# A hybrid decoder layer on one core: other SBUF addresses for the activation tiles of its second part

## The chip, the core and the metric

The kernel runs on one core of a Trainium2 chip. A core has five engines with instruction queues of their own: TensorE (PE in the profile; PEld is its loading of weights), VectorE (DVE), ScalarE (ACT), GpSimd (POOL) and SyncE (SP), which here issues all DMAs. The metric is the device time of one execution in microseconds. Three runs of the kernel before took 3090.01, 3095.93 and 3096.91 us, a median of 3095.93 us.

## What is computed

One layer of a decoder with two groups of heads side by side, on 2048 tokens of width 1024, in float32:

```
u = rmsnorm(h, attn_norm_g);  z = u @ w_in             # 2048x1024 @ 1024x3592
y = concat(mlstm_mixer(z parts), diff_attn_mixer(z parts))
h = h + y @ w_out                                      # 1024x1024
u2 = rmsnorm(h, mlp_norm_g)
h = h + square(relu(u2 @ w_up)) @ w_down               # 1024x4096, 4096x1024
gate = sigmoid(rmsnorm(h, ple_norm_g) @ w_ple_gate)    # 1024x1024
h = h + gate * (p @ w_ple_proj)                        # 256x1024
```

## The kernel before

The program has two parts. `phase1` computes z, the two mixers and, at its end, the product with w_out for the first 512 tokens. `phase2` does the rest in two halves (`hf`) of 1024 tokens, each as two column blocks (`j`) of 512 tokens: the product with w_out, the up and down products of the MLP, the gate.

**Matmuls.** Each float32 operand is split into a rounded part "hi" and a rest "lo" (`split`, L70 to L72: ScalarE writes hi, VectorE or POOL writes lo). `mm3` (L130 to L135) multiplies a pair with three matmuls: L133 hi by hi, L134 weight hi by activation lo, L135 weight lo by activation hi. Every matmul loads 128x128 weights anew and streams its moving operand, in `phase2` 512 columns of an activation tile. One output block takes 24 such matmuls (8 pairs), in the down product 12.

**Tiles.** `cut(buf, base, ...)` takes a piece of a large buffer from element `base` on, 4 bytes each. In `phase2` the weights are pieces of `wbuf` whose blocks of 128 columns lie 512 B apart (L848, L849, L867 to L872). An activation tile is 2 x 512 elements, hi then lo, 4096 B. There are 16 for U (`U_r`) and 16 for act: two in `wbuf` behind the weights, six in `act_r`, eight in `ubuf`. A `Ring` hands them out in turn. U tiles are taken for m, j in that order, so an even number holds column block j = 0 and an odd one j = 1. The `gap` of 96 elements (L851) puts `act_r` and `U_r` at the same address modulo 512 B as `wbuf`; `ubuf` and `wbuf` itself stand so already. By the addresses of the built program, the difference (address of the moving operand less address of the weights that are loaded meanwhile, modulo 512 B) is 0 for every matmul of 512 unbroken columns.

In `phase1` it varies. Its weights are in `wbuf` too, in tiles of 528 elements (2112 B) with two blocks of 264 elements (1056 B) in each. Its `trn` uses them as weights against 4 blocks of 128 columns of U in `ubuf` (768 matmuls, L133 to L135, `bank<-ubuf,wbuf`, until about 1205 us); its `nat` uses U as weights and streams 256 columns of them (`bank<-wbuf,ubuf`).

**Order.** The order of instructions on each engine is set by a scheduler at build time, which works by a timeline of its own; each engine then runs its own list in order. `act_r`, `U_r` and the h tiles lie where `phase1` had its working tiles, so they can be written when those are done; the first write to `act_r` follows the last store of y at 1309 us. The first half's y tiles (L916 to L920, for j = 1 alone, eight of them) are loaded through three temporary buffers (`tmp`) that `fin` (L883) uses too.

Of the kernel before, what the change touches and what calls it, by code (L numbers as in the profile page):

```python
# [8 lines left out]
F32R = mybir.dt.float32r  # L9
# [7 lines left out]
P = 128  # L17
# [6 lines left out]
T1 = 512  # L24
# [16 lines left out]
def hybrid_block(ctx: ExitStack, tc: tile.TileContext, a: dict, out: bass.AP):  # L41
# [48 lines left out]

    phase1(tc, a, wbuf, ubuf, rbuf, banks, yT, hd, qkdr, vdr, ident, identr, identb, masks, ones, negh, split, rstd_col, spread)
    phase2(tc, a, wbuf, ubuf, rbuf, banks, yT, hd, out, split, rstd_col, spread)


def cut(buf, base, *dims, cast=None):
    n = 1
    for d in dims:
        n *= d
    t = buf[:, base:base + n]
    if cast:  # L100
        t = t.bitcast(cast)
    if len(dims) == 2:
        t = t.rearrange("p (a b) -> p a b", a=dims[0])
    elif len(dims) == 3:
        t = t.rearrange("p (a b c) -> p a b c", a=dims[0], b=dims[1])
    return t
# [732 lines left out]
def phase2(tc, a, wbuf, ubuf, rbuf, banks, yT, hd, out, split, rstd_col, spread):  # L839
    nc = tc.nc  # L840
    NJ = T2 // T1
    with ExitStack() as ctx:
        pool = lambda name, bufs=1, **k: ctx.enter_context(tc.tile_pool(name=name, bufs=bufs, **k))
        pc = pool("p2")
# [4 lines left out]
        pw.put("lo", [cut(wbuf, i * 2048 + 1024, KT, P) for i in range(3)])  # L849
        pt.put("tmp", [rbuf[:, 2048 + i * T1:2048 + (i + 1) * T1] for i in range(3)])  # L850
        pc.tile([P, 96], F32, name="gap")  # L851
        more = pc.tile([P, 6, 2 * T1], F32R, name="act_r")
        us = pc.tile([P, 16, 2 * T1], F32R, name="U_r")
        pact.put("U", [cut(us[:, i], 0, 2, T1) for i in range(16)])
        pact.put("act", [cut(wbuf, 6144 + i * 1024, 2, T1) for i in range(2)] + [cut(more[:, i], 0, 2, T1) for i in range(6)] +
                 [cut(ubuf, i * 1024, 2, T1) for i in range(8)])
        acc2 = pc.tile([P, T1], F32, name="acc2")
        pacc.put("acc2", [acc2, rbuf[:, 3584:4096]])
# [48 lines left out]
        for hf in range(NT2):  # L907
# [14 lines left out]
            H, U = [], []  # L922
# [162 lines left out]
```

## Time and profile before

| | us |
|---|---|
| median of three runs | 3095.93 |
| the profiled execution | 3100.62 |
| its span, first to last instruction | 3098.8 |
| TensorE busy | 2979.3 |
| VectorE, ScalarE, POOL busy | 1732.1, 1251.6, 1121.5 |
| mean granted TensorE clock | 0.989 of 2.4 GHz |

The span is divided by the stage tables below in us from its start: `phase2` begins at about 1306 us, its first half ends at about 2063 us and the second half's product with w_out at about 2186 us. The time from one matmul's start to the next one's is shorter than a matmul's printed duration, since matmuls overlap; it is read from the starts of many.

### The profile page before, as it was taken

The page shows a single profiled execution, that of the slowest core. Times are in us where ns is not written, and L with a number is a line of the kernel's source. Part 1 is how long each engine was busy: PE and PEld are TensorE (multiplying, and loading weights), DVE is VectorE, ACT ScalarE, POOL GpSimd, SP SyncE. Part 2 cuts the span into 40 slices and gives each one's busy share as a digit, 9 for nine tenths or more (in the row PEclk, how much of TensorE's full clock was granted, in tenths as well). Part 3 has the DMA queues.
Part 4 walks back from the last instruction along what each step waited for, and adds up shares of the span by engine and source line. Part 5 has one row for each costly group of instructions (what it writes and reads, how often), then busy time and mean ns, then how long its engine had stood idle before and what let it go on. Part 6 is the DMA issues. An engine that isn't in the chain of part 4 may idle for free.

```text
span 3098.8 us, 42670 instructions
## 1 busy us (share of the span) xinstructions
PE 2979.3 (96%) x16136; PEld 2537.9 (82%) x16136; DVE 1732.1 (56%) x3426; ACT 1251.6 (40%) x2836; POOL 1121.5 (36%) x802
## 2 busy tenths in 40 slices
PE   7898999999899999999999999999999999999999
PEld 7788888888888888778888888878788888888877
DVE  7888767667767657375433334463454444333462
ACT  4477666667566666342221211231432222211231
POOL 6667535235533322362222222252632222222341
PEclk9899999999999999999999999999999999999999
DMA  5655534334533332431111111214311111111111
GB/s 162 186 171 158 170 113 123 107 99 125 156 101 104 98 103 75 144 130 49 48 48 48 48 48 48 62 39 137 123 48 48 49 53 49 48 48 48 62 48 68
DMA packets 197806, 278.34 MB, mean 90 GB/s; under 512 B 15584, under 2 KB 145120, under 8 KB 197600
## 3 DMA queue, kind: packets, MB, share of 16 engines
q1 hardware_dynamic: 197600, 275.61, 29.3%
q8 instruction: 127, 2.08, 0.3%
q14 instruction: 79, 0.65, 0.1%
HBM read 235.71 MB, written 39.85 MB: 89 GB/s over the span
## 4 chain that ended last, share of the span: by engine, by line
PE 73%; DVE 13%; ACT 4%; DMA 4%; issue 3%; POOL 3%; SPq 0%; POOLq 0%; ACTq 0%; DVEq 0%
PE bank L133 21%; PE bank L134 21%; PE bank L135 21%; PE bank L824 2%; DMA rbuf<-in_w_in_dram 2%; DVE PP_r L800 2%; PE bank L776 1%; PE bank L779 1%; DVE mxp_r L780 1%; DVE U_r L72 1%; PE bank L812 1%; ACT PP_r L788 1%; POOL wbuf L72 1%; DMA rbuf<-in_x_in_dram 1%; DVE qn_r L727 1%
## 5 line engine op out<-in xcount | busy, mean ns | idle before, releaser
L72 POOL TENSOR_TENSOR wbuf<-rbuf,wbuf 128x512 fp32r<-128x512 f32 (+3 forms) x408 | 733.0, 1802 | 1557.8 <-ACT wbuf L71 1522.5
L71 ACT ACTIVATE wbuf<-rbuf 128x512 fp32r<-128x512 f32 (+3 forms) x410 | 325.9, 799 | 794.5 <-PE bank L134 664.9
L133 PE MATMUL bank<-U_r,wbuf 128*128 128x512 f32 x1280 | 500.0, 391 | 11.9 <-ACT U_r L71 5.8
L134 PE MATMUL bank<-U_r,wbuf 128*128 128x512 f32 x1280 | 499.7, 390 | 1.0 <-DVE U_r L72 1.0
L135 PE MATMUL bank<-U_r,wbuf 128*128 128x512 f32 x1280 | 500.1, 391 | 0.0
L133 PE MATMUL bank<-wbuf,ubuf 128*128 128x256 f32 (+1 forms) x1280 | 382.2, 299 | 18.0 <-DVE wbuf L246 5.6
L973 DVE TENSOR_TENSOR h_r<-bank,h_r 128x512 f32<-128x512 f32 x256 | 176.6, 690 | 394.7 <-PE bank L135 394.7
L133 PE MATMUL bank<-ubuf,wbuf 128*128 128x512 f32 x960 | 380.5, 397 | 5.1 <-ACT ubuf L71 2.7
L135 PE MATMUL bank<-ubuf,wbuf 128*128 128x512 f32 x960 | 377.8, 394 | 0.0
L134 PE MATMUL bank<-ubuf,wbuf 128*128 128x512 f32 x960 | 377.7, 393 | 0.0
L134 PE MATMUL bank<-wbuf,ubuf 128*128 128x256 f32 (+1 forms) x1280 | 375.5, 294 | 1.4 <-DVE wbuf L247 0.9
L135 PE MATMUL bank<-wbuf,ubuf 128*128 128x256 f32 (+1 forms) x1280 | 374.7, 293 | 0.5 <-DVE ubuf L72 0.5
L133 PEld LDWEIGHTS bank<-U_r,wbuf 128*128 128x128 f32 x1280 | 240.7, 188 | 65.4 <-ACT U_r L71 7.0
L134 PEld LDWEIGHTS bank<-U_r,wbuf 128*128 128x128 f32 x1280 | 240.5, 188 | 52.0 <-DVE U_r L72 1.3
L135 PEld LDWEIGHTS bank<-U_r,wbuf 128*128 128x128 f32 x1280 | 240.4, 188 | 50.6 <-issue 1.2
L133 PEld LDWEIGHTS bank<-wbuf,ubuf 128*128 128x128 f32 x1280 | 251.6, 197 | 24.9 <-ACT qn_r L717 5.6
L952 DVE TENSOR_TENSOR rbuf<-rbuf 128x512 f32<-128x512 f32 x64 | 156.5, 2445 | 206.6 <-ACT rbuf L951 206.5
L134 PEld LDWEIGHTS bank<-wbuf,ubuf 128*128 128x128 f32 x1280 | 251.4, 196 | 4.7 <-DVE wbuf L247 1.5
L135 PEld LDWEIGHTS bank<-wbuf,ubuf 128*128 128x128 f32 x1280 | 251.1, 196 | 2.8 <-DVE ubuf L72 0.5
L780 DVE TENSOR_REDUCE mxp_r<-bank 128x1 f32<-128x512 f32 (+3 forms) x320 | 187.0, 602 | 66.7 <-PE bank L779 65.6
L133 PEld LDWEIGHTS bank<-ubuf,wbuf 128*128 128x128 f32 x960 | 181.1, 189 | 45.4 <-ACT ubuf L71 3.9
L788 ACT ACTIVATE PP_r<-bank,mx_r 128x512 f32<-128x512 f32 (+3 forms) x320 | 196.4, 624 | 47.1 <-DVE mx_r L785 42.5
(243 smaller groups left out, 5401.4 us busy)
## 6 DMA issues: line engine op xcount, KB each, us to landing
rbuf<-in_w_in_dram SPq DMA_DIRECT2D x208, 256.0 KB, 2.8
rbuf<-in_w_up_dram SPq DMA_DIRECT2D x64, 512.0 KB, 3.6
rbuf<-in_w_down_dram SPq DMA_DIRECT2D x64, 512.0 KB, 3.5
KT_r<-qk_d SPq DMA_DIRECT2D x40, 512.0 KB, 5.4
qk_d<-kst_r SPq DMA_DIRECT2D x64, 256.0 KB, 3.0
QT_r<-qk_d SPq DMA_DIRECT2D x128, 128.0 KB, 3.8
rbuf<-in_x_in_dram SPq DMA_DIRECT2D x31, 512.0 KB, 4.0
rbuf<-in_w_out_dram SPq DMA_DIRECT2D x24, 512.0 KB, 4.1
```

The costliest lines, as they stand in the source:

```text
L71: nc.scalar.activation(hi, raw, AF.Copy)
L72: eng.tensor_tensor(out=lo, in0=raw, in1=hi.bitcast(F32), op=ALU.subtract)
L133: nc.tensor.matmul(ps, lhsT=lh, rhs=rh, start=(start and i == 0), stop=False)
L134: nc.tensor.matmul(ps, lhsT=lh, rhs=rl, start=False, stop=False)
L135: nc.tensor.matmul(ps, lhsT=ll, rhs=rh, start=False, stop=(stop and i == n - 1))
L727: nc.vector.tensor_tensor(out=qn, in0=qg, in1=rn.unsqueeze(2).broadcast_to([P, 4, 64]), op=ALU.mult)
L780: nc.vector.tensor_reduce(out=mxp[:, m, ci:ci + 1], in_=Sp[:, 0:n], op=ALU.max, axis=AX.X)
L788: nc.scalar.activation(pp[:, 0:n], sps[ci][:, 0:n], AF.Exp, bias=mx[:, m:m + 1], scale=0.125, accum_out=lp[:, m, ci:ci + 1])
L800: nc.vector.scalar_tensor_tensor(out=A[:, 0:n], in0=PP[1][ci][:, 0:n], scalar=sc[:, 0:1], in1=A[:, 0:n], op0=ALU.mult, op1=ALU.add)
L824: nc.tensor.matmul(po, lhsT=ats[kb // 4][:, (kb % 4) * P:(kb % 4 + 1) * P], rhs=VV[kb // 4][:, kb % 4], start=(kb == 0), stop=(kb == i))
L952: nc.vector.tensor_tensor(out=t, in0=t, in1=R[j], op=ALU.mult)
L973: nc.vector.tensor_tensor(out=H[m][j], in0=p, in1=H[m][j], op=ALU.add)
```

## The change

The act tiles in `wbuf` go; `act_r` takes eight instead of six, and `ubuf` keeps its eight. The tiles in `act_r` and `U_r` get offsets in elements: U 16 for even tiles and 64 for odd ones, act 80 for even and 104 for odd ones, which is 64, 256, 320 and 416 B. In the built program the differences of the 7680 matmuls of `phase2` proper are 64 B (1920, U of j = 0), 256 B (1920, U of j = 1), 320 and 416 B (960 each) and 0 (1920, act tiles in `ubuf`). To make room, the scratch for DMA descriptors at the bottom of SBUF shrinks from 16384 to 1024 B, and all tiles move down by 15360 B.

```
-        more = pc.tile([P, 6, 2 * T1], F32R, name="act_r")
-        us = pc.tile([P, 16, 2 * T1], F32R, name="U_r")
-        pact.put("U", [cut(us[:, i], 0, 2, T1) for i in range(16)])
-        pact.put("act", [cut(wbuf, 6144 + i * 1024, 2, T1) for i in range(2)] + [cut(more[:, i], 0, 2, T1) for i in range(6)] +
+        more = pc.tile([P, 8 * 1024 + 128], F32R, name="act_r")
+        us = pc.tile([P, 16 * 1024 + 128], F32R, name="U_r")
+        pact.put("U", [cut(us, (i % 2) * 8192 + (i // 2) * 1024 + (16, 64)[i % 2], 2, T1) for i in range(16)])
+        pact.put("act", [cut(more, (i % 2) * 4096 + (i // 2) * 1024 + (80, 104)[i % 2], 2, T1) for i in range(8)] +
                  [cut(ubuf, i * 1024, 2, T1) for i in range(8)])
...
-    nc = bacc.Bacc("TRN2", target_bir_lowering=False, num_devices=1)
+    nc = bacc.Bacc("TRN2", target_bir_lowering=False, num_devices=1, dynamic_dma_scratch_size=1024)
```

Since the first two act tiles no longer lie in `wbuf`, the scheduler orders the border between the two parts anew. SyncE's list there, as a difference of the changed kernel from the one before (L917 loads a y tile, L529 and L932 x, L870 and L512 weights, L930 h):

```order
@@ -406,7 +406,5 @@
 L710 DMA yT_d_75<-yo_r 128x512
 L536 DMA h_d<-rbuf 128x512
-L917 DMA rbuf<-yT_d_74 128x512
 L529 DMA rbuf<-in_xT_dram 128x512
-L917 DMA rbuf<-yT_d_74 128x512
 L512 DMA rbuf<-in_w_out_dram 128x1024
 L536 DMA h_d<-rbuf 128x512
```

Two loads of y leave the end of `phase1`.

Further on in SyncE's list:

```order
@@ -442,4 +440,5 @@
 L930 DMA h_r<-h_d 128x512
 L932 DMA h_r<-in_xT_dram 128x512
+L917 DMA rbuf<-yT_d_74 128x512 x2
 L870 DMA rbuf<-in_w_out_dram 128x1024
 L930 DMA h_r<-h_d 128x512
```

They come back behind loads of h and ahead of the next weights.

PE at the border, in the kernel before, where the first three output blocks (banks 66, 67 and 68) begin:

```order
6682 L133 MATMUL bank_67<-act_r,wbuf 128x512
6683 L135 MATMUL bank_68<-wbuf 128x512
6684 L133 MATMUL bank_68<-wbuf 128x512
6685 L134 MATMUL bank_68<-wbuf 128x512
6686 L135 MATMUL bank_68<-wbuf 128x512
6687 L133 MATMUL bank_68<-act_r,wbuf 128x512
```

and in the changed one:

```order
6658 L135 MATMUL bank_68<-ubuf,wbuf 128x512
6659 L495 MATMUL bank_67<-ident,ya_r 128x128
6660 L133 MATMUL bank_66<-act_r,wbuf 128x512
6661 L133 MATMUL bank_67<-act_r,wbuf 128x512
6662 L133 MATMUL bank_68<-act_r,wbuf 128x512
6663 L134 MATMUL bank_66<-act_r,wbuf 128x512
```

Before, 18 matmuls of these blocks read y tiles in `wbuf`; now all 72 read `act_r`.

## Rows read from the trace of the kernel before

**Rows 1.** The page: its head, PE's busy time, the chain by engine
```profile
span 3098.8 us, 42670 instructions
...
PE 2979.3 (96%) x16136; PEld 2537.9 (82%) x16136; DVE 1732.1 (56%) x3426; ACT 1251.6 (40%) x2836; POOL 1121.5 (36%) x802
...
PE 73%; DVE 13%; ACT 4%; DMA 4%; issue 3%; POOL 3%; SPq 0%; POOLq 0%; ACTq 0%; DVEq 0%
```

**Rows 2.** Busy time by stage: stretch, length, each engine's busy time, clock, DMA
```profile
1400.00:2062.00 662.00, 662.00 (x2922) 548.15 (x2921) 283.07 (x324) 148.89 (x207) 162.48 (x75) 1.00 0.16 49
...
2300.00:2974.00 674.00, 674.00 (x2975) 558.12 (x2974) 289.22 (x330) 153.03 (x212) 164.99 (x76) 1.00 0.16 49
```

**Rows 3.** Timeline of PE, second part: start us, duration us, engine, line, operation
```profile
1999.79 0.39 PE L133 MATMUL bank<-ubuf,wbuf 128*128 128x512 f32 x1
...
2009.99 0.39 PE L133 MATMUL bank<-ubuf,wbuf 128*128 128x512 f32 x1
```

**Rows 4.** PE's lines from 1999 to 2060 us: busy us, mean ns, idle us before
```profile
L133 PE MATMUL bank<-act_r,wbuf 128*128 128x512 f32 x45 | 17.5, 389 | 0.0
```

**Rows 5.** Timeline of PE, first part: a stretch of wide matmuls, first and last
```profile
495.42 0.40 PE L134 MATMUL bank<-ubuf,wbuf 128*128 128x512 f32 x1
...
500.07 0.40 PE L133 MATMUL bank<-ubuf,wbuf 128*128 128x512 f32 x1
```

**Rows 6.** Timeline of PE after a stall in the second part
```profile
2087.96 0.39 PE L133 MATMUL bank<-U_r,wbuf 128*128 128x512 f32 x1
...
2090.04 0.39 PE L133 MATMUL bank<-U_r,wbuf 128*128 128x512 f32 x1
```

**Rows 7.** PE's lines at 487.20 us, difference 0: mean ns
```profile
L134 PE MATMUL bank<-ubuf,wbuf 128*128 128x512 f32 x1 | 0.4, 389 | 0.0
```

**Rows 8.** PE's lines at 881.12 and 881.50 us, difference 64 B
```profile
L135 PE MATMUL bank<-ubuf,wbuf 128*128 128x512 f32 x1 | 0.4, 394 | 0.0
L133 PE MATMUL bank<-ubuf,wbuf 128*128 128x512 f32 x1 | 0.4, 388 | 0.0
...
L134 PE MATMUL bank<-ubuf,wbuf 128*128 128x512 f32 x1 | 0.4, 392 | 0.0
```

**Rows 9.** PE's lines at 879.30 us, difference 160 B; L134 and L135 read as in rows 8
```profile
L133 PE MATMUL bank<-ubuf,wbuf 128*128 128x512 f32 x1 | 0.4, 391 | 0.0
```

**Rows 10.** Timeline of PE: first and last wide matmul at 64 (modulo 256), at 160
```profile
396.40 0.40 PE L135 MATMUL bank<-ubuf,wbuf 128*128 128x512 f32 x1
...
1201.21 0.39 PE L135 MATMUL bank<-ubuf,wbuf 128*128 128x512 f32 x1
...
394.32 0.39 PE L135 MATMUL bank<-ubuf,wbuf 128*128 128x512 f32 x1
...
1199.59 0.39 PE L134 MATMUL bank<-ubuf,wbuf 128*128 128x512 f32 x1
```

**Rows 11.** Timeline of VectorE at the border: splits of the first half's y tiles
```profile
1248.58 0.68 DVE L72 TENSOR_TENSOR wbuf<-rbuf,wbuf 128x512 fp32r<-128x512 f32 x1
...
1312.30 1.90 DVE L72 TENSOR_TENSOR act_r<-rbuf,act_r 128x512 fp32r<-128x512 f32 x3 [4.98 <-ACT act_r L71]
...
1319.31 1.43 DVE L72 TENSOR_TENSOR act_r<-rbuf,act_r 128x512 fp32r<-128x512 f32 x2 [5.12 <-ACT act_r L71]
```

**Rows 12.** Timeline of PE at the border, in brackets what it waited for
```profile
1309.17 0.50 PE L133 MATMUL bank<-wbuf 128*128 128x512 f32 x1 [1.10 <-ACT wbuf L71]
1312.32 0.73 PE L133 MATMUL bank<-act_r,wbuf 128*128 128x512 f32 x2 [1.02 <-ACT act_r L71]
...
1327.08 0.50 PE L133 MATMUL bank<-wbuf 128*128 128x512 f32 x1 [1.05 <-ACT wbuf L71]
```

**Rows 13.** The page's DMA queues: packets, MB, share of 16 engines
```profile
q1 hardware_dynamic: 197600, 275.61, 29.3%
```

**Rows 14.** Timeline of PE, first part: a stretch of narrow matmuls, first and last
```profile
82.95 0.28 PE L135 MATMUL bank<-wbuf,ubuf 128*128 128x256 f32 x1
...
92.42 0.28 PE L134 MATMUL bank<-wbuf,ubuf 128*128 128x256 f32 x1
```

## The prediction

> **What bounds the kernel now.** I read the page's busy shares and its chain first [rows 1]. The reader is to see that TensorE (PE) is busy for 96% of the span and carries 73% of the chain that ends last. The page warns that a busy PE is not a PE at its peak, so the table by stage comes next [rows 2]. It splits the second part of the program, which begins at about 1306 us. In the two long stretches, 1400 to 2062 us and 2300 to 2974 us, PE is busy for all of 662.00 and 674.00 us at the full granted clock (1.00, the 2.4 GHz level). VectorE, ScalarE and POOL are busy for less than half of either stretch and so have slack. Nothing that feeds PE ends last there. A stretch is as long as its matmuls, and a nanosecond on each matmul is a nanosecond on the span.
>
> What one matmul costs I read from starts, since the durations overlap. In [rows 3] 45 starts pass between 1999.79 and 2009.99 us: 10.20 us / 45 = 226.7 ns each. 512 columns at 2.4 GHz are 213.3 ns, so 13.3 ns are spent beside the columns. A duration (389 ns in [rows 4]) is the second reading: where the next start comes later, the duration is longer by nearly as much. It has the advantage of being printed in nanoseconds.
>
> In this part every activation tile stands at the same address as the weights modulo 512 B: by the built program the difference is 0 for all 7680 matmuls. After the change 1920 have 64 B, 1920 have 256 B, 960 have 320 B and 960 have 416 B. The other 1920 (the act tiles in ubuf) keep 0. So the question is what 226.7 ns becomes at those differences.
>
> **Evidence on the difference, inside the kernel before.** The first part holds 768 matmuls of the same width, 512 columns, whose weights lie in tiles 2112 B apart with halves 1056 B apart. Their difference therefore falls by 32 B every three matmuls and passes through all values. In an undisturbed stretch 20 starts pass in 4.65 us [rows 5]: 232.5 ns, which is more than 5 ns above the second part. So either the difference or the stepping of it costs something. A second witness is what follows a stall in the second part, at difference 0 throughout: nine starts in 2.08 us, 231.1 ns each, before the steady value returns [rows 6]. The cost of a matmul thus depends on a state that it inherits, and at difference 0 that state settles on 226.7 ns within some nine matmuls.
>
> At single differences (assigned from the addresses in the built program), the durations say the following. At 0 a matmul in the middle of such a stretch already shows the steady 389 ns [rows 7]. At 64 B three in a row show 394, 388 and 392 ns [rows 8], a mean of 391.3 and so 2.3 ns over the steady value. At 160 B they show 394, 391 and 392 ns [rows 8, 9], 3.3 ns over. Over all such matmuls, 74 at 64 or 320 B and 90 at 160 or 416 B (first and last of each in [rows 10]), the starts are 231.6 and 231.0 ns apart. Taken alone, 64 and 320 B give 231.6 each, so I count a difference modulo 256: 256 as 0, 320 as 64 and 416 as 160.
>
> **The change part by part.**
>
> 1. *U tiles at 64 B (1920 matmuls).* The lower end is the 2.3 ns of the triple; the upper end is 231.6 - 226.7 = 4.9 ns, as if nothing ever settled. These matmuls come in runs of 24, long enough to settle but entered from another state each time. I take 3.3 ns, nearer to the triple: 1920 x 3.3 = 6.3 us.
> 2. *U tiles at 256 B (1920 matmuls).* These are as at 0: no cost once settled.
> 3. *Act tiles at 320 B (960 matmuls).* As item 1: 960 x 3.3 = 3.2 us.
> 4. *Act tiles at 416 B (960 matmuls).* Ends 3.3 and 4.3 ns (231.0 - 226.7); runs of 12 or fewer settle least, so I take the upper: 4.1 us.
> 5. *Settling again on tiles whose difference counts as 0.* In PE's new order the difference returns to 0 or 256 from another value 225 times. One return costs between nothing ([rows 7], steady at once) and 9 x 4.4 = 40 ns ([rows 6]). I take 13 ns, a third, because most returns come from states already near: 2.9 us, ends 0 and 9 us.
> 6. *The border between the parts.* Before, two of the eight y tiles of the first half went into wbuf, which was free early. VectorE split the first of them at 1248.58 us, and only six were left for the border, in two batches that begin at 1312.30 and 1319.31 us [rows 11]. PE did the 18 matmuls of the two early ones around 1309 us, before the first act_r tile let it go on at 1312.32 us [rows 12]. After, all eight lie in act_r, which opens only there. So 18 x 0.227 = 4.1 us of matmuls leave a stretch in which PE waited anyway. Also, the last two loads stand on SP's queue behind several loads of h_r and need temporary buffers that the second batch frees. Queued behind that on PE are the groups of the same stretch, and behind their sums VectorE's additions and the splits that make U. One more batch after 1319.31 us lands some 7 us later, at about 1326 us (the distance of the two batches). Before, PE waited at 1327.08 us for weights in any case. Ends 0 (that wait absorbs it) and 8 us (a whole batch handed on); I take the 4 us.
> 7. *Edits at nothing.* The DMA scratch shrinks and every tile below it moves by 15360 B, 30 x 512, so no difference in the first part changes. All the data moves through one queue [rows 13], and every DMA of it is issued by SyncE, none by POOL; I take it that none of them uses the scratch. Were that wrong, waits before DMAs would show it, at a few us for each that is late. The second half's y and p tiles only change buffers.
>
> Sum: 6.3 + 3.2 + 4.1 + 2.9 + 4 = 20.5 us. The profiled execution took 3100.62 us (span 3098.8 us and 1.8 around it) and would become 3121.1. The median of the three timed runs is 4.7 us below the profiled one, so the forecast is 3095.9 + 20.5 = 3116 us, 0.66% slower. The ends add up to 3095.9 + 4.4 + 2.2 + 3.2 = 3106 and 3095.9 + 14.1 + 4.1 + 9 + 8 = 3131 us.
>
> **The rivals.**
>
> *A, the difference does not matter.* The wide matmuls of the first part differ from those of the second in one more way: their moving operand is four blocks of 128 columns, 4096 B apart, instead of one row of 512. If the 5 ns are the price of the blocks, the second part keeps 226.7 ns, and only the border's 0 to 4 us remain: 3096 to 3100 us, within 0.2%. For it: no wide matmul at another difference with an unbroken operand is in the trace. Against it: at difference 0 the blocked ones take the steady 389 ns [rows 7], so blocks alone cost nothing there. The Trainium skill, "TensorE: Matmul & The Clock Gate", section "What happens when you issue a matmul", speaks for A: TensorE reads its moving operand and its weights through two independent ports, so that loading weights takes nothing from a running matmul. By that rule no address could matter, and [rows 5] against [rows 3] disagrees with it unless the blocks explain it.
>
> *B, 0 is a dear difference.* The narrow matmuls of the first part (256 columns, unbroken, moving operand stepping through the differences) start every 118.4 ns: 80 in 9.47 us [rows 14], or 11.7 ns beside the columns' 106.7. The steady wide one has 13.3. If the new differences cost 11.7 too, each of the 3840 matmuls that move off 0 gains 1.7 ns: 6.5 us, and with a border that is absorbed 3089 us. It decides if the steady start-to-start time at 64 B falls below 226.7 ns. Against it: wide matmuls at 64 and 160 B do not show it.
>
> *C, no settling at all.* With a new difference every 12 or 13 matmuls (586 changes in 7680) the state may never settle, at the 231.6 ns of item 1 everywhere: 3840 x 4.9 = 18.8 us, with the 9 us of item 5 and 4 to 8 us at the border 3128 to 3132 us.
>
> **How the numbers follow.** Forecast 0.60, A 0.17, B 0.11, C 0.12. A measurement of this kernel can tell about 0.2%, 6.2 us, from no change: the three runs before spread over 6.9 us. Slower by over that is the forecast and C, 0.72; within it A, 0.17; faster B, 0.11. The range runs from 3094 us, below A, to 3130 us, the lower half of C; B and the upper half of C stay out, 0.17 together.
>
> **What would show it.** In the profile after, the durations of the matmuls out of U_r should rise above 389 ns in alternate groups of 24: about 392 at 64 B, 389 at 256 B after the first few. Those out of act_r should have a mean of 392 to 394, and those out of ubuf one of 390. The stage 1400 to 2062 us should be some 6 us longer with PE still busy throughout, and the clock granted at 1.00. At the border PE's wait before the first act_r matmul should grow, and the third batch of y tiles should be split near 1326 us. The forecast is wrong if act_r and U_r stay at 389 ns (A), go below it (B), or if idle time of PE appears inside the long stretches, which no item here foresees.

## The result, and the profile after

| | before | after |
|---|---|---|
| runs, median (us) | 3096.42 | 3121.25 |
| ratio, with its 95% interval | | 1.0075 (1.0061 to 1.0089) |
| span of the profiled execution (us) | 3098.8 | 3124.5 |
| PE busy (us) | 2979.3 | 3003.1 |
| mean granted TensorE clock | 0.989 | 0.987 |

By the ratio the change makes the kernel 0.75% slower, which is 23 us (19 to 28); the two medians of four runs are 24.8 us apart. The forecast was 20.5 us. The page after, its head, PE's busy time, the chain and the three groups of U matmuls (busy us, mean ns of one, idle us before):

```profile
span 3124.5 us, 42667 instructions
...
PE 3003.1 (96%) x16136; PEld 2542.0 (81%) x16136; DVE 1733.0 (55%) x3426; ACT 1253.1 (40%) x2836; POOL 1123.5 (36%) x802
...
PE 73%; DVE 13%; ACT 4%; DMA 4%; issue 3%; POOL 2%; SPq 0%; ACTq 0%; POOLq 0%; DVEq 0%
...
L133 PE MATMUL bank<-U_r,wbuf 128*128 128x512 f32 x1280 | 505.2, 395 | 6.2 <-ACT U_r L71 5.7
L134 PE MATMUL bank<-U_r,wbuf 128*128 128x512 f32 x1280 | 502.1, 392 | 4.4 <-DVE U_r L72 4.4
L135 PE MATMUL bank<-U_r,wbuf 128*128 128x512 f32 x1280 | 504.6, 394 | 0.0
```

Against [rows 1] the engines' shares and the chain are the same to a per cent, and only PE is busier by more than 2 us: by 24 us, with as many matmuls. The two long stretches of the second part, by PE (length, busy, matmuls started, clock, DMA):

```profile
1400.00:2062.00 662.00, 662.00 (x2891) 1.00 0.16 49
```
```profile
2300.00:2974.00 674.00, 674.00 (x2923) 548.68 (x2922) 279.97 (x320) 147.14 (x203) 155.77 (x68) 1.00 0.16 49
```

PE is again busy throughout and its clock is again 1.00, but it starts 31 and 52 matmuls fewer than in [rows 2]. Nothing waits; each matmul takes longer. By tile, PE's lines from 1400 to 2060 us:

```profile
L133 PE MATMUL bank<-U_r,wbuf 128*128 128x512 f32 x466 | 183.2, 393 | 0.0
L135 PE MATMUL bank<-U_r,wbuf 128*128 128x512 f32 x466 | 182.5, 392 | 0.0
L134 PE MATMUL bank<-U_r,wbuf 128*128 128x512 f32 x466 | 181.4, 389 | 0.0
L133 PE MATMUL bank<-ubuf,wbuf 128*128 128x512 f32 x256 | 99.6, 389 | 0.0
...
L134 PE MATMUL bank<-act_r,wbuf 128*128 128x512 f32 x239 | 94.4, 395 | 0.0
L135 PE MATMUL bank<-act_r,wbuf 128*128 128x512 f32 x238 | 94.0, 395 | 0.0
L133 PE MATMUL bank<-act_r,wbuf 128*128 128x512 f32 x239 | 93.9, 393 | 0.0
```

All groups of this stretch read 389 ns before, for example:

```profile
L133 PE MATMUL bank<-U_r,wbuf 128*128 128x512 f32 x463 | 180.1, 389 | 0.0
...
L134 PE MATMUL bank<-act_r,wbuf 128*128 128x512 f32 x189 | 73.5, 389 | 0.0
```

Now act_r is dearest, U_r is between, and ubuf, which kept difference 0, is at 389 here, where its runs are 192 matmuls long. In the second long stretch, from 2300 to 2974 us, it takes turns with act_r every six matmuls, and there it is not:

```profile
L134 PE MATMUL bank<-ubuf,wbuf 128*128 128x512 f32 x238 | 93.9, 394 | 0.0
L135 PE MATMUL bank<-ubuf,wbuf 128*128 128x512 f32 x238 | 93.6, 393 | 0.0
L133 PE MATMUL bank<-ubuf,wbuf 128*128 128x512 f32 x238 | 93.3, 392 | 0.0
```

So a matmul pays for its own difference, and for the one before it. Both are seen in one pair of groups of 24, from the first starts of the group at 64 B, of that at 256 B and of the next:

```profile
1675.57 0.40 PE L133 MATMUL bank<-U_r,wbuf 128*128 128x512 f32 x1
...
1681.08 0.40 PE L133 MATMUL bank<-U_r,wbuf 128*128 128x512 f32 x1
...
1686.57 0.40 PE L133 MATMUL bank<-U_r,wbuf 128*128 128x512 f32 x1
```

That is 5.51 us / 24 = 229.6 ns and 5.49 us / 24 = 228.8 ns. The durations in the settled part of each, 1678.2 to 1681.0 us and then 1683.7 to 1686.5 us:

```profile
L135 PE MATMUL bank<-U_r,wbuf 128*128 128x512 f32 x5 | 2.0, 392 | 0.0
L134 PE MATMUL bank<-U_r,wbuf 128*128 128x512 f32 x5 | 1.9, 388 | 0.0
L133 PE MATMUL bank<-U_r,wbuf 128*128 128x512 f32 x4 | 1.6, 394 | 0.0
```
```profile
L134 PE MATMUL bank<-U_r,wbuf 128*128 128x512 f32 x5 | 1.9, 389 | 0.0
L135 PE MATMUL bank<-U_r,wbuf 128*128 128x512 f32 x5 | 1.9, 389 | 0.0
L133 PE MATMUL bank<-U_r,wbuf 128*128 128x512 f32 x4 | 1.6, 389 | 0.0
```

At 64 B the settled state is the triple 394, 388, 392 ns of [rows 8], to the nanosecond. At 256 B it is the 389 of difference 0, but only after some ten matmuls. Averaged by place over the 63 groups of 24 at 256 B that follow a group at 64 B, the starts are 234.0, 231.3, 232.6, 235.3, 225.3, 230.5, 234.2, 227.9, 231.3 and 230.0 ns apart and then 226.8.

A difference does not always settle on the same value. Of the 75 groups of 24 at 64 B whose second half has no wait in it, 72 end at 228.9 ns and three at 233.3. These three, which begin at 2421.86, 2598.9 and 2776.0 us, all follow six matmuls out of act_r at 416 B. The second half of the first one (2424.8 to 2427.3 us) reads

```profile
L135 PE MATMUL bank<-U_r,wbuf 128*128 128x512 f32 x5 | 2.0, 397 | 0.0
L133 PE MATMUL bank<-U_r,wbuf 128*128 128x512 f32 x4 | 1.6, 397 | 0.0
L134 PE MATMUL bank<-U_r,wbuf 128*128 128x512 f32 x4 | 1.6, 397 | 0.0
```

So the state in which a group begins can last to its end.

From the starts of all wide matmuls of the second part that follow each other without a wait (7,622 steps below 245 ns), against 226.7 ns:

| tile, difference | steps | mean ns | excess, us |
|---|---|---|---|
| U_r, 64 B | 1896 | 229.7 | 5.8 |
| U_r, 256 B | 1893 | 228.5 | 3.4 |
| act_r, 320 B | 947 | 230.5 | 3.6 |
| act_r, 416 B | 957 | 234.2 | 7.2 |
| ubuf, 0 B | 1929 | 229.0 | 4.4 |

The sum is 24.4 us; the same sum for the kernel before is 0.9 us, so 23.5 us are the change's. The border between the parts makes up the rest. VectorE's splits of the y tiles there, and PE (start, duration, what it waited for in brackets):

```profile
1309.96 1.99 DVE L72 TENSOR_TENSOR act_r<-rbuf,act_r 128x512 fp32r<-128x512 f32 x3 [4.68 <-ACT act_r L71]
1316.65 2.18 DVE L72 TENSOR_TENSOR act_r<-rbuf,act_r 128x512 fp32r<-128x512 f32 x3 [4.70 <-ACT act_r L71]
1323.36 1.34 DVE L72 TENSOR_TENSOR act_r<-rbuf,act_r 128x512 fp32r<-128x512 f32 x2
```
```profile
1309.98 1.65 PE L133 MATMUL bank<-act_r,wbuf 128*128 128x512 f32 x3 [5.32 <-ACT act_r L71]
1311.43 0.63 PE L134 MATMUL bank<-act_r,wbuf 128*128 128x512 f32 x1
1311.86 0.63 PE L135 MATMUL bank<-act_r,wbuf 128*128 128x512 f32 x1
```

Against [rows 11] and [rows 12] there are three batches instead of two, and PE waits 5.32 us in one piece where it had waited 1.10, done a little work and waited 1.02. Then its starts are 0.43 us apart: 512 columns at 1.2 GHz are 0.427 us, so the clock is at the lower of its two levels. The clock granted from 1310 to 1320 us, before and after (length, PE busy, matmuls, clock):

```profile
1310.00:1320.00 10.00, 8.98 (x39) 1.00 0.84 244
```
```profile
1310.00:1320.00 10.00, 10.00 (x35) 0.79 0.88 305
```

The first part ends earlier or later by up to 10 us from one profile to the next, even where its order is the same. Stages are therefore compared from a common point, the last matmul of the mixers (L824, at 1299.11 us before and 1297.07 us after; at 1289.13 us in the run below with the order of before and the smaller scratch). From it to the 2000th hi by hi matmul (L133, counted from 0) the kernel before takes 296.1 us and the changed one 302.0. From there to the last L133 it is 1498.3 and 1520.1 us. Together that is 27.7 us more. The profiled execution of the changed kernel was the slowest of its four runs (3126.66 us).

### The profile page after: what moved, and what is told of

The parts are those of the page before. It is cut to its first block, busy times and chain, and to the rows that moved or that the text cites. A ratio compares the mean times of both kernels' runs of the same rounds, so it can differ in the third digit from the quotient of the medians.

```text
span 3124.5 us, 42667 instructions
## 1 busy us (share of the span) xinstructions
PE 3003.1 (96%) x16136; PEld 2542.0 (81%) x16136; DVE 1733.0 (55%) x3426; ACT 1253.1 (40%) x2836; POOL 1123.5 (36%) x802
## 4 chain that ended last, share of the span: by engine, by line
PE 73%; DVE 13%; ACT 4%; DMA 4%; issue 3%; POOL 2%; SPq 0%; ACTq 0%; POOLq 0%; DVEq 0%
PE bank L133 21%; PE bank L135 21%; PE bank L134 21%; PE bank L824 2%; DMA rbuf<-in_w_in_dram 2%; DVE U_r L72 1%; DVE PP_r L800 1%; DVE mxp_r L780 1%; PE bank L779 1%; PE bank L776 1%; PE bank L812 1%; ACT PP_r L788 1%; DMA rbuf<-in_x_in_dram 1%; POOL wbuf L72 1%; DVE qn_r L727 1%
## 5 line engine op out<-in xcount | busy, mean ns | idle before, releaser
L133 PE MATMUL bank<-U_r,wbuf 128*128 128x512 f32 x1280 | 505.2, 395 | 6.2 <-ACT U_r L71 5.7
L134 PE MATMUL bank<-U_r,wbuf 128*128 128x512 f32 x1280 | 502.1, 392 | 4.4 <-DVE U_r L72 4.4
L135 PE MATMUL bank<-U_r,wbuf 128*128 128x512 f32 x1280 | 504.6, 394 | 0.0
L133 PE MATMUL bank<-wbuf,ubuf 128*128 128x256 f32 (+1 forms) x1280 | 380.3, 297 | 17.0 <-ACT ubuf L277 5.9
L133 PE MATMUL bank<-ubuf,wbuf 128*128 128x512 f32 x960 | 381.2, 398 | 6.2 <-ACT ubuf L71 3.5
L135 PE MATMUL bank<-ubuf,wbuf 128*128 128x512 f32 x960 | 379.4, 396 | 0.0
L134 PE MATMUL bank<-ubuf,wbuf 128*128 128x512 f32 x960 | 379.0, 395 | 0.0
L134 PE MATMUL bank<-wbuf,ubuf 128*128 128x256 f32 (+1 forms) x1280 | 373.6, 292 | 0.9 <-DVE wbuf L247 0.9
L135 PE MATMUL bank<-wbuf,ubuf 128*128 128x256 f32 (+1 forms) x1280 | 373.2, 292 | 0.5 <-DVE ubuf L72 0.5
L133 PEld LDWEIGHTS bank<-U_r,wbuf 128*128 128x128 f32 x1280 | 241.3, 189 | 60.1 <-ACT U_r L71 7.1
L134 PEld LDWEIGHTS bank<-U_r,wbuf 128*128 128x128 f32 x1280 | 241.6, 189 | 59.1 <-DVE U_r L72 5.2
L135 PEld LDWEIGHTS bank<-U_r,wbuf 128*128 128x128 f32 x1280 | 241.5, 189 | 55.8 <-issue 1.2
L133 PEld LDWEIGHTS bank<-wbuf,ubuf 128*128 128x128 f32 x1280 | 249.5, 195 | 24.0 <-ACT ubuf L277 5.8
L133 PE MATMUL bank<-act_r,wbuf 128*128 128x512 f32 x640 | 252.1, 397 | 5.3 <-ACT act_r L71 5.3
L135 PE MATMUL bank<-act_r,wbuf 128*128 128x512 f32 x640 | 253.4, 396 | 0.6 <-POOL wbuf L72 0.6
L134 PE MATMUL bank<-act_r,wbuf 128*128 128x512 f32 x640 | 253.3, 396 | 0.0
L134 PEld LDWEIGHTS bank<-wbuf,ubuf 128*128 128x128 f32 x1280 | 249.5, 195 | 3.9 <-DVE wbuf L247 1.5
L135 PEld LDWEIGHTS bank<-wbuf,ubuf 128*128 128x128 f32 x1280 | 249.3, 195 | 2.9 <-DVE ubuf L72 0.8
```

Source lines behind the costliest of these rows:

```text
L133: nc.tensor.matmul(ps, lhsT=lh, rhs=rh, start=(start and i == 0), stop=False)
L134: nc.tensor.matmul(ps, lhsT=lh, rhs=rl, start=False, stop=False)
L135: nc.tensor.matmul(ps, lhsT=ll, rhs=rh, start=False, stop=(stop and i == n - 1))
```

## Experiments

**Do the differences alone do it?** Theory D, that of the prediction: a matmul costs by its address difference, modulo 256 B. Rival R: the new order, the tiles' new places and the smaller scratch cost it, and the differences nothing. Rival S: no difference is dear in itself, only changing it. Rival P: it is the place of the tile within 512 B that counts, not its difference to the weights. Four kernels keep everything of the changed one but the offsets. Three have its order on every engine too; in the fourth (weights and tiles moved together) the scheduler put a few of PE's matmuls and two loads elsewhere at the border.

All offsets 0 (e1_zero):

```
-  (16, 64)[i % 2]      # U
+  0
-  (80, 104)[i % 2]     # act
+  0
```

> The changed kernel with all four offsets at 0 elements: same tiles, same small scratch, same order of every engine, address difference 0 everywhere. Theory D (the difference between the moving operand's address and that of the weights loaded meanwhile, modulo 256 B, sets the spacing of matmuls): 3096 us within 4 us, durations of 389 ns out of U_r, act_r and ubuf, spacing 226.7 ns. Rival R (the new order at the border between the parts, the loss of the wbuf tiles or the scratch costs the time): 3115 to 3125 us, the offsets being no cause.

All tiles, ubuf included, at 64 B (e2_all64), and all at 256 B (e3_all256):

```
-  (16, 64)[i % 2] ... (80, 104)[i % 2] ... cut(ubuf, i * 1024, 2, T1)
+  16              ... 16               ... cut(ubuf, i * 1024 + 16, 2, T1)
```

> All 32 activation tiles of the second part, those in ubuf too, at a difference of 64 B, so that it never changes from group to group. Theory D: the cycle of three spacings seen in the changed kernel's U tiles of j = 0 (226.7, 229.5, 231.2, mean 229.1 ns) everywhere: 7680 x 2.4 = 18.6 us over the kernel before, 3115 us, without the cost of settling. Rival R: 3121 us as for any offsets. Rival S (only the changing of the difference costs, no value of it is dear by itself): 3096 us.

> As the run before with 256 B in place of 64. Theory D with a period of 256 B: 3096 us within 4 us, durations 389 ns, since 256 counts as 0 and nothing changes from group to group. If the period is 512 B: a spacing other than 226.7 ns and 3100 us or more. Rival R: 3121 us.

All tiles at 64 B and the weights too, so that every place moves and the difference stays 0 (e4_shift64):

```
-  pw.put("hi", [cut(wbuf, i * 2048, KT, P) for i in range(3)])
+  pw.put("hi", [cut(wbuf, i * 2048 + 16, KT, P) for i in range(3)])
```

> Weights of the second part and all activation tiles moved by 64 B together: the difference is 0, the addresses of the moving tiles are those of the run with 64 B everywhere. Theory D: 3096 us within 4 us, 389 ns. Rival P (the place of the moving tile itself modulo 512 B decides, not its difference to the weights): as with 64 B everywhere, 3115 us.

| kernel | median us (before) | ratio | mean start to start, ns | to the 2000th, us | from there, us |
|---|---|---|---|---|---|
| all 0 | 3101.67 (3097.05) | 1.0014 (1.0000 to 1.0028) | 226.8 | 299.6 | 1498.0 |
| all 64 B | 3119.65 | 1.0073 (1.0058 to 1.0088) | 228.9 | 302.2 | 1512.9 |
| all 256 B | 3100.25 | 1.0007 (0.9997 to 1.0016) | 226.8 | 300.2 | 1497.8 |
| weights and tiles + 64 B | 3100.39 | 1.0012 (1.0002 to 1.0021) | 226.8 | 299.8 | 1501.8 |

With all differences 0 the long stretches are those of before, so R falls as the main cause. A line of U_r from 1400 to 2060 us in that run, to be held against the one of the changed kernel above:

```profile
L133 PE MATMUL bank<-U_r,wbuf 128*128 128x512 f32 x458 | 178.2, 389 | 0.0
```

Theory D gave 3096 us within 4 for the first, third and fourth; all three came out a little above that, since it left out the border. For all tiles at 256 B the time alone does not decide (3100 us or more was the sign of a period of 512 B); the 226.8 ns do. With everything at 64 B the difference never changes and still costs, which S cannot give. PE's U lines from 1400 to 2060 us with all at 64 B show the settled triple:

```profile
L133 PE MATMUL bank<-U_r,wbuf 128*128 128x512 f32 x468 | 184.4, 394 | 0.0
L135 PE MATMUL bank<-U_r,wbuf 128*128 128x512 f32 x469 | 183.8, 392 | 0.0
L134 PE MATMUL bank<-U_r,wbuf 128*128 128x512 f32 x469 | 182.0, 388 | 0.0
```

Moving weights and tiles together costs nothing of the kind, so P falls. Beside that, 3.5 to 4 us stay with the new order at the border in the three with a cheap difference (the next to last column, 296.1 before).

**The two halves of the change, apart.** U alone at 64 and 256 B, act_r at 0 (e5_u_only), and act_r alone at 320 and 416 B, U at 0 (e12_act_only):

```
-  (80, 104)[i % 2]     # act, in e5_u_only
+  0
```
```
-  (16, 64)[i % 2]      # U, in e12_act_only
+  0
```

> The changed kernel with act_r back at difference 0; U keeps 64 and 256 B, so half of the matmuls still change and the runs of 24 alternate. Theory S (a difference has its own steady interval, 226.7 ns at 0 and 256, 228.9 at 64, and after every change some ten matmuls are dearer): U at 64 about 229.7 ns mean, U at 256 about 228.4, act and ubuf near 227.5 as they are entered from U at 64 or 256 alternately; 5.8 + 3.3 + 2 = 11 us over the kernel with all differences 0: about 3112 us (ratio to before 1.005). Rival N (only a matmul's own difference counts, changing it costs nothing): 1920 x 2.3 ns = 4.4 us, U at 256 at 226.7 ns: about 3105 us (ratio 1.0025).

> The changed kernel with U back at difference 0 and act_r still at 320 and 416 B; the counterpart of the run with U alone. Theory S (steady cost by difference modulo 256, 64 at 2.2 ns and 160 at 7.5 ns, and dear matmuls after each change): act_r at 320 B 230.5 ns and at 416 B 234.2 ns as in the changed kernel, ubuf, which is entered from act_r, about 229 ns, U 227; 3.6 + 7.2 + 4.4 and up to 1 for U = 15 to 16 us over the kernel with all differences 0, about 3117 us (ratio 1.006). Rival P (the prediction's sizes: 416 B at 4.3 ns, ubuf hardly anything): 3.2 + 4.1 + 2 = 9 us, about 3110 us (ratio 1.004). Rival Q (act at 416 B was dear because the state came from U at 64 B): 416 B near 229 ns, 3108 us.

U alone: 3109.48 us, ratio 1.0041 (1.0030 to 1.0052). U at 64 B is at 229.6 ns (5.5 us over 226.7), U at 256 B at 228.5 (3.5 us), act_r at 226.7, ubuf at 226.9 (0.5 us): 9.6 us. Act alone: 3114.48 us, ratio 1.0061 (1.0041 to 1.0082). The 320 B are at 230.5 ns (3.6 us), the 416 B at 234.2 (7.2 us), ubuf at 228.8 (4.1 us), U at 226.9 (0.8 us): 15.7 us. The halves add up to 25.3 us against 24.4 in the changed kernel, and each stands over the kernels with one fixed cheap difference (mean ratio 1.0011 of the first, third and fourth above and the one with 0 and 256 B below) by about its own sum: 0.30%, 9 us, and 0.50%, 15 us. N falls in the first, since U at 256 B pays for following U at 64 B. Theory S of that run had act_r and ubuf a little too dear (227.5 ns), and with them the time (3112 us). In the second both rivals of that run fall: act at 416 B costs nearly twice the forecast, whatever U does.

**What is each difference worth once it has settled?** U at two other differences, in runs of 24 that are long enough to settle; act_r at 0.

```
-  (16, 64)[i % 2]
+  (8, 32)[i % 2]       # 32 and 128 B; (24, 40): 96 and 160 B; (48, 56): 192 and 224 B
```

> U at 32 B (even tiles) and 128 B (odd tiles), act_r at 0. To be read: the interval in positions 12 to 23 of each run of 24, where it has settled. T1 (cost grows with the distance from the nearest multiple of 256): 32 B about 227.8 ns, 128 B about 236, run about 3125 us. T2 (cost grows with the difference up to 256): 227.8 and 231.5, about 3116. T3 (every difference but 0 and 256 settles on 229, and 416 B is dear only because its runs are short): 229 for both, about 3116. T4 (128 B is as good as 0): 128 B at 226.7. Rival B (0 is a dear one): one of them below 226.7 ns, under 3097 us.

> U at 96 B (even tiles) and 160 B (odd tiles), act_r at 0; positions 12 to 23 of each run of 24. 160 is 416 modulo 256, which here gets runs of 24 and not 12. T1 (distance from the nearest multiple of 256): both about 234 ns, run about 3130 us. T2 (grows with the difference): 230.3 and 234, about 3125. T3 (416 B was dear for its short runs): both settle on 229, about 3116. Rival B: one below 226.7 ns.

> U at 192 B (even tiles) and 224 B (odd tiles), act_r at 0; positions 12 to 23 of each run of 24. T1 (distance from the nearest multiple of 256): 192 B about 229 ns, 224 B about 228, run about 3111 us. T2 (grows with the difference): 236 and 237, about 3140. T3: both 229, about 3116. Rival B: one below 226.7 ns.

The single runs took 3129.41, 3127.83 and 3125.31 us, with the clock at 1.00 from 1400 to 2060 us in each. Mean start to start in places 12 to 23 of the groups:

| difference mod 256, B | 0 | 32 | 64 | 96 | 128 | 160 | 192 | 224 |
|---|---|---|---|---|---|---|---|---|
| settled, ns | 226.7 | 233.3 | 228.9 | 233.4 | 233.2 | 234.5 | 233.3 | 233.4 |

PE's lines in the second half of a group at 96 B (1677.0 to 1679.8 us) and of the next at 160 B (1682.6 to 1685.4 us), in the run with these two:

```profile
L135 PE MATMUL bank<-U_r,wbuf 128*128 128x512 f32 x5 | 2.0, 399 | 0.0
L134 PE MATMUL bank<-U_r,wbuf 128*128 128x512 f32 x4 | 1.6, 394 | 0.0
L133 PE MATMUL bank<-U_r,wbuf 128*128 128x512 f32 x4 | 1.6, 392 | 0.0
```
```profile
L134 PE MATMUL bank<-U_r,wbuf 128*128 128x512 f32 x5 | 2.0, 398 | 0.0
L135 PE MATMUL bank<-U_r,wbuf 128*128 128x512 f32 x5 | 2.0, 396 | 0.0
L133 PE MATMUL bank<-U_r,wbuf 128*128 128x512 f32 x4 | 1.6, 396 | 0.0
```

None of the forms T1 to T4 is right. It is neither a distance nor a ramp: 0 is best, 64 B is 2.2 ns over it, and the six others are 6.5 to 7.8 ns over it, 128 B no better than 32. None of them beats 0, so B falls for matmuls of this width and for multiples of 32 B; other offsets were not tried. Each of the six was seen in one pairing only. Since 64 B has a second cycle at 233.3 ns, near the value of five of these six, whether they have a cheaper one is not known.

**Is it the change of the address, or of the address modulo 256?** U and act tiles at 0 (even) and 256 B (odd) (e9_0_256):

```
-  (16, 64)[i % 2] ... (80, 104)[i % 2]
+  (0, 64)[i % 2]  ... (0, 64)[i % 2]
```

> The changed kernel with U and act tiles at 0 (even) and 256 B (odd): the difference changes as often as in the changed kernel, but never modulo 256. Theory S256 (256 B and 0 are one and the same; what costs is a change of the difference modulo 256): every wide matmul of the second part at 226.7 to 226.8 ns, no dear ones after a change, about 3100 us as with all differences 0 (ratio 1.001). Rival C (any change of address difference costs, whatever its size): some ten dear matmuls of 4 to 5 ns after each change, 4 to 6 us more, about 3105 us.

3100.49 us, ratio 1.0011 (1.0001 to 1.0021). U is at 226.8 ns at either difference, and the first matmul of U at 256 B after a change is at 226.9, where it was at 234.0 in the changed kernel. By these times 0 and 256 B are the same to PE.

**The scratch, and the border.** The kernel before with the smaller scratch alone, where every engine's order is that of before (e10_scratch):

```
-    nc = bacc.Bacc("TRN2", target_bir_lowering=False, num_devices=1)
+    nc = bacc.Bacc("TRN2", target_bir_lowering=False, num_devices=1, dynamic_dma_scratch_size=1024)
```

> The kernel before with the DMA scratch cut to 1024 B and nothing else; every engine's order stays. Theory O (the 3.3 us between the 1500th and the 2000th hi by hi matmul, 395.1 us before and 398.4 with all differences 0, are the new order at the border): 395 us between those two, time as before, 3096 to 3097 us (ratio 1.000). Rival K (the smaller scratch or the moved addresses slow transfers): 398 us between the two, about 3100 us (ratio 1.001).

3097.05 us, ratio 0.9998 (0.9988 to 1.0007), and 295.8 us from the last L824 to the 2000th hi by hi matmul, as before. So scratch and moved addresses cost nothing that the runs can tell, and the 299.5 to 300.2 us of the four kernels with differences of 0 or 256 B alone belong to the new order: 3.5 to 4 us. Their border reads nearly as in the changed kernel; PE with all differences 0:

```profile
1304.53 1.65 PE L133 MATMUL bank<-act_r,wbuf 128*128 128x512 f32 x3 [5.13 <-ACT act_r L71]
```

From the last hi by hi matmuls of the first part on (1193 to 1591 us, answering to 1200 to 1595 before) PE's waits there add up to 15.9 us against 13.7, and after the last L824 18 starts, instead of 8, are between 0.38 and 0.6 us from the next, as at the lower clock. That is 2.2 us and 10 x 0.2 = 2 us, together about the measured cost.

After this point a single profile scatters too. This kernel, unchanged there, takes 1501.3 us to the end, and the one before 1498.3. A stage of one profile is good to some 3 us.

**A version with difference 0 everywhere.** The kernel before, its first part's weights spread so that the difference is 0 modulo 256 there too (e11_first; the smaller scratch makes room). The scheduler orders the end of the first part anew here too, PE's list from 1236 to 1299 us, so it is not a change of addresses alone:

```
-    wbuf = shared.tile([P, 2 * NW * 528], F32R, name="wbuf")
+    wbuf = shared.tile([P, 2 * NW * 640], F32R, name="wbuf")
...
-            pw.put(tag, [cut(wbuf, base + i * 528, 2, 264) for i in range(NW)])
+            pw.put(tag, [cut(wbuf, base + i * 640, 2, 320) for i in range(NW)])
```

> The kernel before with the scratch cut as well, and the weight tiles of the first part spread from 2112 to 2560 B with halves 1280 B apart, so that the difference is 0 modulo 256 for every matmul of the first part too. Theory D (the difference sets the interval of a matmul in the first part as well): the 768 wide ones fall from about 232.5 to 227 ns, 3.8 us at most, where PE ends last; the narrow ones (118.4 ns for 256 columns) fall by up to the same 5 ns or not at all: 3082 to 3094 us. Rival W (in the first part other engines and the transfers end last, so PE's gain becomes waiting): 3094 to 3099 us.

3095.94 us, ratio 0.9997 (0.9987 to 1.0007): no gain. The matmuls moved as D says, but not all the way. The first part's wide ones, undisturbed, first and 21st start:

```profile
961.15 0.40 PE L134 MATMUL bank<-ubuf,wbuf 128*128 128x512 f32 x1
...
965.69 0.39 PE L133 MATMUL bank<-ubuf,wbuf 128*128 128x512 f32 x1
```

4.54 us / 20 = 227 ns against 232.5 in [rows 5]. By the mean of the 622 undisturbed steps it is 229.2 against 232.1 ns, since after a wait or a group of other matmuls the first ones are dear at difference 0 too: 1.8 us gained. The narrow ones, 80 starts as in [rows 14]:

```profile
82.81 0.28 PE L135 MATMUL bank<-wbuf,ubuf 128*128 128x256 f32 x1
...
92.39 0.28 PE L134 MATMUL bank<-wbuf,ubuf 128*128 128x256 f32 x1
```

9.58 us / 80 = 119.8 ns against 118.4, and by the mean of some 2,750 undisturbed steps 119.2 against 118.2: 2.8 us lost. At 256 columns 0 is 1 ns dearer than the mean of a stepping difference. Neither D nor W is decided by the time: loss and gain nearly cancel, the order is not that of before (297.6 us from the last L824 to the 2000th hi by hi matmul, against 296.1), and the first part scatters by 10 us.

## Why the prediction held, and where it did not

It held in its cause and its sign, and the time came out within its range. Two of its terms, 4 and 5, were far too small; that the total is still within 3 us of the 23 measured is in part luck, since the traces add up to more than the timed runs show. The parts, in us:

| item | forecast | measured |
|---|---|---|
| 1, U at 64 B | 6.3 | 5.8 |
| 3, act at 320 B | 3.2 | 3.6 |
| 4, act at 416 B | 4.1 | 7.2 |
| 2 and 5, settling on 256 and on 0 | 2.9 | 3.4 + 4.4 = 7.8 |
| 6, the border | 4 | 3.5 to 4 |
| 7, scratch and places | 0 | 0 (ratio 0.9998) |

- **Item 1 and item 3 were right**, and for the reason given: the triple of [rows 8] was the settled state at 64 B in nearly all groups, and the runs with all tiles at 64 B and with U alone show it. To count 320 as 64 and 256 as 0 was right as well.
- **Item 4 was mis-sized.** 416 does count as 160. But its price was taken from a mean over matmuls of the first part that were each at 160 B for three in a row [rows 10], with the argument that short runs settle least and so cost most. That assumes that settled is always cheaper. At 160 B it is the reverse: 231.0 ns is the unsettled value, and the settled one is 234.5. Three matmuls in a row had shown 394, 391 and 392 ns, where the settled state has 396 to 398.
- **Item 5 was mis-sized.** The 13 ns for a return rested on "most returns come from states already near". They do not. Of the 225 returns 66 go to U at 256 B, from 64 B: such a group starts with ten matmuls of 225.3 to 235.3 ns, 45 ns too many in all (62 groups without a wait), just over the upper end of 40 ns from the stall in [rows 6]. The other 159 go to ubuf and cost 4.4 us, 28 ns each, mostly in runs that end after six matmuls. That stall was the right row, taken whole: from its first start on, the steps are 229, 233, 236, 224, 231, 236, 228, 233 and 231 ns, and the second to tenth step at 256 B after 64 B are the same within 2.5 ns.
- **Item 6 was right in size and place.** The third batch came at 1323.36 us (forecast 1326) and the wait before the first act_r matmul grew from 1.02 to 5.32 us. Not foreseen was that about half of its cost is the lower clock after that wait. Also, in the changed kernel some of the dear matmuls of this stretch disappear in its waits: they cost 3.5 us there, but it takes only 2.4 us more than with all differences 0 (302.0 against 299.6). So the border must be read in the kernels with one cheap difference.
- **The sum.** By the traces the items come to 23.5 + 3.5 = 27 us, and the stages of the one profile, of the slowest run, differ by 27.7; the timed runs differ by 23 (19 to 28). The forecast of 20.5 is lower because items 4 and 5 were. Among the signs named beforehand, act_r reads 393 to 395 ns in the first long stretch (392 to 394 forecast), and ubuf 389 there but 392 to 394 in the second (390 forecast).
- **Rival A** fell. All tiles of the second part are unbroken rows, and 64 B of difference alone takes them from 226.8 to 228.9 ns. The rule that the Trainium skill, "TensorE: Matmul & The Clock Gate", section "What happens when you issue a matmul", gives, that moving operand and weights are read through independent ports, would leave addresses without effect; it does not hold here to within 1 to 3 per cent, since the settled time differs by 2 to 8 ns of 227 by these two addresses alone. What in the chip makes the difference no run shows. Blocks as such cost nothing, as [rows 7] said: with difference 0 in the first part they take 227 ns once settled.
- **Rival B** fell for wide matmuls; no difference beats 0. Its row was true for what it showed, narrow matmuls are cheaper while the difference steps, but it does not carry from 256 columns to 512.
- **Rival C** fell: U settles, at 64 B after four matmuls (but for the three groups that stay at 233.3 ns) and at 256 B after ten. Its end for item 5, 9 us, was near all the same.

That PE's starts go by the difference between the two addresses is shown. Why 0 and 64 B are the good ones, why 64 B has two settled values, and whether it is the weights loaded meanwhile or the matmul's own that count (both have the same address modulo 256 in this part), stays open and was not tried.

## What to carry to other kernels

Where PE is busy throughout at full clock, read start-to-start times and not busy shares, and keep the moving operand of wide matmuls at one address difference to the weights, 0 modulo 256 B: here that was worth 2 to 8 ns of 227 on each. A price that is read from operations which never stay in one state is not the price of the settled state, and may lie on either side of it. In this kernel a stall in the same loop was a fair price for a return to the settled state.

## What was not expected of the hardware

The settled start-to-start time of a 512-column float32 matmul with its own weight load depends on the difference of the two addresses modulo 256 B: 226.7 ns at 0, 228.9 at 64 B, 233.2 to 234.5 at the six other multiples of 32 B. It also depends on what came before, since three groups at 64 B stayed at 233.3 ns. After a change it wanders through 225 to 238 ns for up to ten matmuls, nearly the same way each time: the first eight values of U at 256 B after 64 B in the changed kernel and in the run with U alone agree, as means, within 1.2 ns. At difference 0 both widths leave about 13 ns beside their columns (226.7 - 213.3 = 13.4 and, by the one stretch, 119.8 - 106.7 = 13.1).
